# Which pairs of an input projection take seven products, and which stage forms their weight sums

## The chip, the cores and the metric

The kernel runs on one core of a Trainium2 chip. The metric is the device time of one execution in microseconds (us); a figure for a kernel is the median of its runs. The engines are TensorE (PE; its weight loads are listed apart as PEld), VectorE (DVE), ScalarE (ACT), GpSimd (POOL) and SyncE (SP). Each engine works through its own instructions in order and waits on semaphores for the others. Here SP issues the loads from memory and POOL most of the stores.

## The reference, cut to what matters

One inference step of a hybrid decoder over 1024 prompt tokens and 8 decoded tokens, model width 2048: one pooling layer (A), a shared key and value projection, one attention layer (B), all in float32. The change touches the input projection of layer A, `x @ w_in` with a weight of 2048 x 4096. Its first 2048 columns, here called the means, go through trailing means over 2, 4, 8 and 16 tokens in four channel groups of 512; its last 2048 columns are the gates.

```python
def multiscale_pool(u, prefix, pos):
    ...
    for g, w in enumerate(POOL_WINDOWS):
        ...
        outs.append((hi[..., sl] - lo) / cnt)
    pooled = jnp.concatenate(outs, axis=-1) - extf[:, P:]
    return pooled.astype(u.dtype), ext[:, -P:]

def pool_layer(x, prefix, pos, w_in, w_grp, scale, w_out, g_ln, b_ln):
    B, T, _ = x.shape
    z = x @ w_in
    u, gate = z[..., :D_POOL], z[..., D_POOL:]
    d, new_state = multiscale_pool(u, prefix, pos)
    d = jnp.einsum('btgc,gce->btge', d.reshape(B, T, N_POOL_GROUPS, POOL_GROUP), w_grp)
    d = d.reshape(B, T, D_POOL) * scale
    y = (d * jax.nn.silu(gate)) @ w_out
    return layer_norm(ALPHA * x + y, g_ln, b_ln), new_state
```

## The kernel before

**Stages.** The tokens go in two chunks (`c`): the first 512, then the other 512 with the 8 decoded ones (520). `PHASES` lists the stages: `ai` (input projection of A) for chunk 0 and 1, `ao` (output projection) for both, then `bi` and `bo` for layer B. `ai` of chunk 0 is cut in two entries: group 0 alone, and groups 1 to 3. Within a group come two pairs of means, two pairs of gates, and two group halves (`group_half`, the small product with `w_grp`, L1092, evicted by DVE at L1109).

**Exact products.** Each float32 operand is split in an upper half (a cast on ACT, L483 for weights, L773 for x) and a lower half (a subtraction on DVE, L498 for weights, L782 for x). A product takes three matmuls: upper by upper, upper by lower, lower by upper (L662, L663, L664 in seven-product form; L690, L691, L692 in plain form). A weight piece is 128x1024, 512 KB, loaded by SP.

**Plain and seven products.** A pair is two blocks of 128 output channels over all 2048 inputs and one chunk of tokens, so four weight pieces a11, a12, a21, a22. In plain form (`unit`, L1153 evicts a unit of the means on ACT, L1140 one of the gates) it is 4 entries of 24 matmuls with 512 columns. In the form of Strassen and Winograd (`seven`) it is 7 entries of 24 matmuls with half the columns, 256 or 260. Those need four sums of weight pieces and four sums of x tiles (T1 to T4). `PLAIN` names the stages in plain form: group 0 of `ai` in chunk 0, and half of `bi` in chunk 0. All others take seven products.

**Where the sums come from.** In a plain stage `plain_pair` loads the four pieces and afterwards forms the four weight sums on DVE (L288), which POOL stores (L289) for the second chunk. In a seven-product stage of chunk 0 `first_pair` forms them ahead of use (L341) from five loads (a22 twice) and stores them (L342). In chunk 1 `next_pair` loads seven pieces, four of them stored sums. The T tiles of the first chunk are formed from the plain stage's x tiles by `t_first` (L740 to L743, four operations for each quarter) at steps 3, 6, 9 and 12; two of the seven x operands are views of the plain tiles. The rest, ten pieces, are cast and split by `x_make` and `x_cast`, which `x_tick` calls at each step. `x_begin` starts this for the next stage; for the first seven-product stage it is called ahead of group 0's gates.

**Order.** One Python program writes the instructions, and a rule at the end (`in_order`) holds PE, DVE and ACT to the order in which they were written. `begin` looks ahead of each entry: loads 7 entries ahead, casts 4, lower halves 3 (5, 4 and 3 in a plain stage). A step (`end`) is one entry, or half of one in a plain stage. It runs what was due at that step (`at`), then `x_tick`, then now and then one step of background work (`side`). Background work is here `t_gen`, which loads x and writes T tiles of the next chunk (L830 to L833), `sum_gen`, which forms weight sums for the output projection, and the layer norms; how often it runs is counted in steps from the start of the program (`self.i / self.every`). In `ai` of chunk 0 five such steps are also put into each group's second pair of gates.

**A pool tile.** When a unit of the means is done, ACT copies it (L1153, or within `seven` the lines L601 to L635), DVE forms the trailing mean (L1038, L1046, L1049), ACT casts the result (L270) and DVE takes its lower half (L271).

The functions that the change touches, with the line numbers of the profile:

## Time and profile before

| | |
|---|---|
| median of 3 runs | 2331.8 us (2331.34 to 2332.02) |
| profiled execution, its own time | 2329.57 us |
| its span, first to last instruction | 2327.8 us |
| mean granted TensorE clock | 0.998 |
| busy share of the span | PE 99%, PEld 95%, DVE 83%, ACT 59%, POOL 9% |
| memory traffic | 669.26 MB, mean 288 GB/s |

A row of a timeline gives start, duration, engine, line, operation, output and input with their shapes, and in brackets how long the engine had been idle ahead of it and what ended that. Starts of successive rows on one engine lie a little closer than the durations, so the distance between starts is what an operation costs a busy engine. A window row gives busy time and instruction count of each engine, the granted TensorE clock (1.00 is full), the mean busy share of the DMA engines and GB/s. A list of waits gives who waited for whom, total, times, and the longest.

### The profile page before, as it was taken

What the parts mean: (1) busy time and instruction counts of PE and PEld (TensorE: products, weight loads), DVE (VectorE), ACT (ScalarE), POOL (GpSimd) and SP (SyncE); (2) the same over time, 40 slices, a digit from 0 to 9 for tenths busy, and PEclk for the clock granted to TensorE, in tenths of its full rate; (3) what the DMA queues carried; (4) which work ended last, traced back from release to release, by engine and by line L of the source; (5) the groups of instructions that cost most, each with busy time, mean ns of one, the idle gap of its engine ahead of it and who ended that gap; (6) DMA issues with size and microseconds to landing.
All of it is one profiled execution on the core that took longest, in us unless ns stands there. A gap on an engine that the chain in (4) does not pass through costs nothing. (4 is left out here: it accounts for less than half of the span.)

```text
span 2327.8 us, 49646 instructions
## 1 busy us (share of the span) xinstructions
PE 2297.9 (99%) x19960; PEld 2201.7 (95%) x19960; DVE 1922.3 (83%) x2382; ACT 1362.7 (59%) x2502; POOL 204.0 (9%) x384
## 2 busy tenths in 40 slices
PE   8999999999999999999999999999999999999997
PEld 6899999999999999999888899999999999999997
DVE  8788898777878878878898898897777767889897
ACT  4444455544546546655465566785766778656565
POOL 0111110010000000000111111100000000010001
PEclk9999999999999999999999999999999999999999
DMA  8668789988889988898789766788777758799785
GB/s 293 220 232 303 258 301 355 332 304 290 310 304 318 343 282 318 317 359 311 275 312 372 265 240 229 245 317 286 251 258 234 237 175 299 250 362 376 264 323 185
DMA packets 252216, 669.26 MB, mean 288 GB/s; under 512 B 25904, under 2 KB 106704, under 8 KB 251984
## 3 DMA queue, kind: packets, MB, share of 16 engines
q1 hardware_dynamic: 206512, 501.00, 63.4%
q0 software_dynamic: 45472, 165.07, 18.2%
q8 instruction: 156, 2.56, 0.4%
q14 instruction: 76, 0.62, 0.1%
HBM read 470.88 MB, written 185.59 MB: 282 GB/s over the span
## 5 line engine op out<-in xcount | busy, mean ns | idle before, releaser
L662 PE MATMUL pD<-m,m 128*128 128x260 f32 (+1 forms) x4752 | 1345.7, 283 | 1.8 <-ACT pD L601 0.9
L664 PE MATMUL pD<-m,m 128*128 128x260 f32 (+1 forms) x4752 | 1339.6, 282 | 5.5 <-DVE m L498 5.4
L663 PE MATMUL pD<-m,m 128*128 128x260 f32 (+1 forms) x4752 | 1340.0, 282 | 0.6 <-DVE m L782 0.6
L662 PEld LDWEIGHTS pD<-m,m 128*128 128x128 f32 x4752 | 895.5, 188 | 9.6 <-issue 5.5
L664 PEld LDWEIGHTS pD<-m,m 128*128 128x128 f32 x4752 | 895.9, 189 | 7.2 <-DVE m L498 7.1
L663 PEld LDWEIGHTS pD<-m,m 128*128 128x128 f32 x4752 | 895.6, 188 | 1.3 <-DVE m L782 0.8
L498 DVE TENSOR_TENSOR m<-m,m 128x1024 fp32r<-128x1024 f32 x674 | 814.6, 1220 | 96.2 <-ACT m L483 62.6
L483 ACT CAST m<-m 128x1024 fp32r<-128x1024 f32 x674 | 703.3, 1048 | 208.2 <-DVE m L341 84.9
L690 PE MATMUL pD<-m,m 128*128 128x512 f32 x448 | 179.8, 401 | 8.1 <-ACT m L773 8.1
L691 PE MATMUL pD<-m,m 128*128 128x512 f32 x448 | 177.4, 396 | 0.5 <-DVE m L782 0.5
L692 PE MATMUL pD<-m,m 128*128 128x512 f32 x448 | 177.4, 396 | 0.0
L782 DVE TENSOR_TENSOR m<-m,m 128x1024 fp32r<-128x1024 f32 (+1 forms) x120 | 147.0, 1227 | 10.3 <-ACT m L773 8.7
L773 ACT CAST m<-m 128x1024 fp32r<-128x1024 f32 (+1 forms) x120 | 125.8, 1052 | 14.0 <-DVE m L498 4.8
L341 DVE TENSOR_TENSOR m<-m,m 128x1024 f32<-128x1024 f32 x88 | 107.6, 1223 | 9.1 <-DMA m<-in_wia 6.8
L635 ACT COPY m<-pD 128x260 f32<-128x260 f32 (+1 forms) x83 | 31.0, 373 | 140.5 <-PE pD L664 140.2
L690 PEld LDWEIGHTS pD<-m,m 128*128 128x128 f32 x448 | 84.8, 189 | 29.4 <-ACT m L773 8.1
L623 DVE TENSOR_TENSOR m<-pD,m 128x260 f32<-128x260 f32 (+1 forms) x86 | 36.2, 421 | 83.8 <-ACT pD L622 76.3
L691 PEld LDWEIGHTS pD<-m,m 128*128 128x128 f32 x448 | 84.9, 189 | 20.0 <-DVE m L782 1.0
L692 PEld LDWEIGHTS pD<-m,m 128*128 128x128 f32 x448 | 84.8, 189 | 19.7
L1818 ACT ACTIVATE m<-m,sm 128x128 f32<-128x128 f32 x256 | 99.3, 391 | 0.0
L1092 PE MATMUL pD<-m,m 128*128 128x260 f32 (+1 forms) x528 | 91.2, 323 | 0.0
L1092 PEld LDWEIGHTS pD<-m,m 128*128 128x128 f32 x528 | 79.4, 188 | 8.1
(248 smaller groups left out, 2113.1 us busy)
## 6 DMA issues: line engine op xcount, KB each, us to landing
m<-in_wia SPq DMA_DIRECT2D x124, 512.0 KB
m<-in_wib SPq DMA_DIRECT2D x120, 512.0 KB
swia<-m POOLq DMA_DIRECT2D x64, 512.0 KB, 4.9
m<-swia SPq DMA_DIRECT2D x64, 512.0 KB
m<-swoa SPq DMA_DIRECT2D x64, 512.0 KB
swib<-m POOLq DMA_DIRECT2D x64, 512.0 KB, 5.1
m<-swib SPq DMA_DIRECT2D x64, 512.0 KB
m<-swob SPq DMA_DIRECT2D x56, 512.0 KB
```

What stands on the lines that cost most here:

```text
L341: self.nc.vector.tensor_add(s[out].a[:, :1024], s[x].a[:, :1024], s[y].a[:, :1024])
L483: self.nc.scalar.copy(hi.r[:, :1024], self.stream[self.cast].src().a[:, :1024])
L498: self.nc.vector.tensor_sub(lo.r[:, :1024], s.src().a[:, :1024], hi.a[:, :1024])
L662: nc.tensor.matmul(ps[:, :TH], wh[:, s], h, start=new and k == 0, stop=False, skip_group_check=on)
L663: nc.tensor.matmul(ps[:, :TH], wh[:, s], l, start=False, stop=False, skip_group_check=on)
L664: nc.tensor.matmul(ps[:, :TH], wl[:, s], h, start=False, stop=k == 7, skip_group_check=on)
L690: nc.tensor.matmul(ps[:], wh[:, s], h, start=par == 0 and k == 0, stop=False)
L691: nc.tensor.matmul(ps[:], wh[:, s], l, start=False, stop=False)
L692: nc.tensor.matmul(ps[:], wl[:, s], h, start=False, stop=par == 1 and k == 7)
L773: self.nc.scalar.copy(h.r[:, :n], s.a[:, :n])
L782: self.nc.vector.tensor_sub(l.r[:, :n], s.a[:, :n], h.a[:, :n])
L1092: nc.tensor.matmul(ps[:, : cs.stop - cs.start], ws[:, s], d[:, cs], start=f0 and k == 0, stop=l0 and k == 3,)
```

## The change

The first entry of `PHASES` now stands for the means of group 0 alone: parts are numbered 2g for the means of group g and 2g + 1 for its gates, so the first stage is part 0 and the second parts 1 to 7. The means of group 0 stay plain, by `bare_pair`, which forms no sums. Group 0's gates become the first two pairs of the second stage, with seven products and `first_pair`, which stores their sums for chunk 1 as for the other groups. In chunk 1 the means of group 0, its first two pairs, no longer find stored sums; `first_pair` with `keep=False` forms them there from five loads and stores nothing. `phase_ai` is cut into `means` and `gates`. The quarters of T tiles are formed at steps 3, 5, 7 and 9, and `x_begin` for the second stage is called at step 10 of the first stage's 16, with `turn` set, so that `x_tick` handles two pieces a step.

```diff
--- before.py
+++ after.py
@@ -48,7 +48,7 @@
 N_CST = K_MP + P + 1
 
 PHASES = (
-    ("ai", 0, (0, 1)), ("ai", 0, (1, 4)), ("ai", 1, (0, 4)), ("ao", 0, None), ("ao", 1, None), ("bi", 0, (0, 4)),
+    ("ai", 0, (0, 1)), ("ai", 0, (1, 8)), ("ai", 1, (0, 8)), ("ao", 0, None), ("ao", 1, None), ("bi", 0, (0, 4)),
     ("bi", 0, (4, 8)), ("bi", 1, (0, 8)), ("bo", 0, None), ("bo", 1, None),
 )
 PHASE_OF = {"x": "ai", "g": "ao", "h": "bi", "o": "bo"}
@@ -324,7 +324,12 @@
             ent[i].loads.insert(0, lambda: self.sums(name, q))
         return ent
 
-    def first_pair(self, name, q):
+    def bare_pair(self, name, q):
+
+        a11, a12, a21, a22 = self.quads(name, q)
+        return [self.lone(a) for a in (a11, a12, a21, a22)]
+
+    def first_pair(self, name, q, keep=True):
 
         a11, a12, a21, a22 = self.quads(name, q)
         ws = self.ws[name][q]
@@ -339,12 +344,13 @@
                 if out not in s:
                     s[out] = self.mem.full(1024)
                 self.nc.vector.tensor_add(s[out].a[:, :1024], s[x].a[:, :1024], s[y].a[:, :1024])
-                self.nc.gpsimd.dma_start(ws[:, i, :], s[out].a[:, :1024])
+                if keep:
+                    self.nc.gpsimd.dma_start(ws[:, i, :], s[out].a[:, :1024])
 
             return go
 
         def free(*ks):
-            return [lambda k=k: s.pop(k).free(k != "c") for k in ks]
+            return [lambda k=k: s.pop(k).free(keep and k != "c") for k in ks]
 
         ent = lambda k, loads, make, after: Entry(loads, make, lambda: s[k], after)
         return {
@@ -374,10 +380,17 @@
             if seven and c == 0:
                 pr = lambda name, q: (lambda f: [f[i] for i in ORDER7])(self.first_pair(name, q))
             if kind == "ai":
-                for g in range(*part):
-                    for q in (2 * g, 2 * g + 1, 8 + 2 * g, 9 + 2 * g):
-                        w += pr("wia", q)
-                    for h in range(2):
+                for n in range(*part):
+                    g, gates = divmod(n, 2)
+                    for q in (8 * gates + 2 * g, 8 * gates + 2 * g + 1):
+                        if n:
+                            w += pr("wia", q)
+                        elif c == 0:
+                            w += self.bare_pair("wia", q)
+                        else:
+                            f = self.first_pair("wia", q, False)
+                            w += [f[i] for i in ORDER7]
+                    for h in range(2 if gates else 0):
                         w.append(self.lone(io["wg"][g][:, h * 1024 : (h + 1) * 1024]))
             elif kind == "bi":
                 if part[0] == 0:
@@ -1133,18 +1146,19 @@
 
         return box, z(0), z(1)
 
-    def phase_ai(self, c, gs, nxt):
+    def phase_ai(self, c, parts, nxt):
         nc, io = self.nc, self.io
         T = CHUNKS[c][1]
         TH = T // 2
         silu = lambda dst, ps: nc.scalar.activation(dst, ps, AF.Silu)
-        for g in gs:
+
+        def means(g, end):
             ext = es = None
             if T > TP:
                 es = self.mem.half(T)
                 ext = es.a[:, :512].rearrange("p (i b w) -> p i b w", i=4, b=NDEC)
                 nc.sync.dma_start(ext, io["st"][:, 4 * g : 4 * g + 4])
-            dd, sg = {}, {}
+            dd = self.dd = {}
             for i in range(4):
                 if not self.strassen:
 
@@ -1153,6 +1167,7 @@
                         nc.scalar.copy(U.a[:, NST : NST + T], ps[:])
                         self.at(1, lambda: self.pool_tile(c, 4 * g + i, U, None, dd))
 
+                    self.last = end and i == 3
                     self.unit(done)
                 elif i % 2 == 0:
                     us = {}
@@ -1170,6 +1185,7 @@
                         self.at(n + 4, lambda: self.pool_tile(c, 4 * g + i + 1, us[1], ext, dd))
 
                     self.pair(c, z(0), z(1), done)
+            self.last = False
             if ext is not None:
 
                 def put(es=es, ext=ext, g=g):
@@ -1177,35 +1193,31 @@
                     es.free()
 
                 self.at(8, put)
-            for i in range(4):
-                if g == gs[-1] and i == 0:
-                    self.x_begin(nxt)
-                if not self.strassen:
-
-                    def done(ps, i=i):
-                        if i % 2 == 0:
-                            sg[i // 2] = self.mem.full(2 * T)
-                        silu(sg[i // 2].a[:, (i % 2) * T : (i % 2 + 1) * T], ps[:])
-
-                    self.last = g == gs[-1] and i == 3
-                    self.unit(done)
-                elif i % 2 == 0:
-                    box, z0, z1 = self.two(T)
-
-                    def done(i=i, box=box):
-                        s = box["s"]
-                        silu(s.a[:, TH : 2 * T], s.a[:, TH : 2 * T])
-                        sg[i // 2] = s
-
-                    if c == 0 and i == 2:
-
-                        for n in range(0, 10, 2):
-                            self.at(n, lambda: self.side and self.side_step())
-                    self.last = g == gs[-1] and i == 2
-                    self.pair(c, z0, z1, done, silu)
+
+        def gates(g, end):
+            sg = {}
+            if end:
+                self.x_begin(nxt)
+            for i in (0, 2):
+                box, z0, z1 = self.two(T)
+
+                def done(i=i, box=box):
+                    s = box["s"]
+                    silu(s.a[:, TH : 2 * T], s.a[:, TH : 2 * T])
+                    sg[i // 2] = s
+
+                if c == 0 and i == 2:
+
+                    for n in range(0, 10, 2):
+                        self.at(n, lambda: self.side and self.side_step())
+                self.last = end and i == 2
+                self.pair(c, z0, z1, done, silu)
             self.last = False
             for h in range(2):
-                self.group_half(c, g, h, dd, sg)
+                self.group_half(c, g, h, self.dd, sg)
+
+        for n in parts:
+            (gates if n % 2 else means)(n // 2, n == parts[-1])
         if T > TP:
             nc.sync.dma_start(io["npp"], self.carry)
 
@@ -2116,8 +2128,8 @@
             if n == 3:
                 self.prep_to(2)
         for j in range(4):
-            self.at(3 + 3 * j, lambda j=j: self.t_first(j))
-        self.at(13, lambda: setattr(self, "x0", None))
+            self.at(3 + 2 * j, lambda j=j: self.t_first(j))
+        self.at(10, lambda: setattr(self, "x0", None))
         nc.vector.tensor_scalar(
             self.nsink, self.nsink, -1.0, None, op0=ALU.mult
         )
@@ -2160,7 +2172,8 @@
             self.at(7, lambda: setattr(self, "turn", False))
             self.at(13, lambda: setattr(self, "lock", False))
             if n == 0:
-                pass
+                self.at(10, lambda: self.x_begin(1))
+                self.at(10, lambda: setattr(self, "turn", True))
             elif (kind, c) == ("ai", 0):
                 add(("x", 1, False), self.t_gen(("x", 1)))
                 self.room = 99
```

What moves is shown at three places. The lines of the code before are 13 lower than those after from L495 on (L498 is L511, L782 is L795, L773 is L786, L483 is L496, L270 and L271 stay, L341 is L346, L1109 is L1122, L1153 is L1167).

On DVE, around the end of group 0's means, before: the sums of the plain stage (L288) between lower halves of plain gates, and the first x pieces of the seven-product stage (L782).

```order
L498 TENSOR_TENSOR m_83_586<-m_71_508,m_78_548 128x1024
L288 TENSOR_TENSOR m_71_508<-m_67_464,m_71_508 128x1024
L271 TENSOR_TENSOR m_85_604<-m_81_580,m_85_604 128x512
L288 TENSOR_TENSOR m_67_464<-m_54_380,m_67_464 128x1024
L498 TENSOR_TENSOR m_89_628<-m_76_544,m_84_588 128x1024
L288 TENSOR_TENSOR m_54_380<-m_54_380,m_71_508 128x1024
L782 TENSOR_TENSOR m_91_646<-m_79_562,m_86_621 128x1024
L288 TENSOR_TENSOR m_62_424<-m_54_380,m_62_424 128x1024
L782 TENSOR_TENSOR m_93_664<-m_80_564,m_92_648 128x1024
L498 TENSOR_TENSOR m_96_670<-m_82_584,m_90_630 128x1024
```

And after, from the last operation of the third unit's pool tile (L1062) on:

```order
L1062 TENSOR_SCALAR m_72_494<-m_72_494,m_69_460 128x512
L511 TENSOR_TENSOR m_76_504<-m_63_422,m_71_466 128x1024
L346 TENSOR_TENSOR m_62_420<-m_58_380,m_62_420 128x1024
L346 TENSOR_TENSOR m_58_380<-m_58_380,m_63_422 128x1024
L271 TENSOR_TENSOR m_78_524<-m_72_494,m_78_524 128x512
L795 TENSOR_TENSOR m_79_527<-m_67_443,m_73_498 128x1024
L795 TENSOR_TENSOR m_80_529<-m_68_445,m_74_500 128x1024
L795 TENSOR_TENSOR m_83_547<-m_41_286,m_81_531 128x1024
L795 TENSOR_TENSOR m_84_549<-m_54_370,m_82_533 128x1024
L511 TENSOR_TENSOR m_89_559<-m_58_380,m_77_510 128x1024
L795 TENSOR_TENSOR m_91_588<-m_40_285,m_85_551 128x1024
L795 TENSOR_TENSOR m_92_590<-m_53_369,m_86_553 128x1024
```

The sums of the first gate pair (L346) and the x pieces (L795, two by two) now stand here, next to the means' pool tiles, and the split L271 has a sum directly ahead of it.

On ACT at the same place, before: the fourth unit's eviction (L1153) behind the split of the third unit's tile (L270).

```order
L483 COPY m_73_512<-m_67_464 128x1024
L270 COPY m_74_526<-m_70_504 128x512
L1153 COPY m_75_542<-pD_461 128x512
L483 COPY m_78_548<-m_71_508 128x1024
L1030 COPY area<-m_75_542 128x15
L483 COPY m_84_588<-m_76_544 128x1024
L270 COPY m_85_604<-m_81_580 128x512
L773 COPY m_86_621<-m_79_562 128x1024
L1140 ACT_TABLE_LOAD
```

And after, from the third unit's eviction (L1167) on:

```order
L1167 COPY m_69_460<-pD_377 128x512
L496 COPY m_71_466<-m_63_422 128x1024
L1043 COPY area<-m_69_460 128x15
L786 COPY m_73_498<-m_67_443 128x1024
L786 COPY m_74_500<-m_68_445 128x1024
L496 COPY m_77_510<-m_58_380 128x1024
L270 COPY m_78_524<-m_72_494 128x512
L786 COPY m_81_531<-m_41_286 128x1024
L786 COPY m_82_533<-m_54_370 128x1024
```

Ahead of the split L270 there are now two x casts (L786) and the cast of a weight sum (L496, `m_58_380`, which the second sum of the fence above writes, in the row behind `m_62_420`).

On DVE at the end of chunk 0's `ai`, where the group halves of group 3 are evicted (L1109, from `pD`), before:

```order
L498 TENSOR_TENSOR m_490_4082<-m_466_3933,m_485_4046 128x1024
L782 TENSOR_TENSOR m_492_4112<-m_460_3896,m_487_4074 128x1040
L1109 TENSOR_SCALAR m_495_4118<-pD_4086,prm,m_433_3698 128x512
L1109 TENSOR_SCALAR m_495_4118<-pD_4099,prm,m_433_3698 128x512
L498 TENSOR_TENSOR m_497_4124<-m_471_3967,m_491_4084 128x1024
L782 TENSOR_TENSOR m_499_4154<-m_465_3930,m_493_4114 128x1040
L1109 TENSOR_SCALAR m_503_4162<-pD_4128,prm,m_470_3965 128x512
L1109 TENSOR_SCALAR m_503_4162<-pD_4141,prm,m_470_3965 128x512
```

And after:

```order
L511 TENSOR_TENSOR m_500_4218<-m_478_4074,m_495_4183 128x1024
L346 TENSOR_TENSOR m_488_4143<-m_487_4141,m_488_4143 128x1024
L795 TENSOR_TENSOR m_502_4247<-m_475_4068,m_497_4211 128x1040
L511 TENSOR_TENSOR m_505_4255<-m_482_4107,m_501_4220 128x1024
L346 TENSOR_TENSOR m_487_4141<-m_482_4107,m_487_4141 128x1024
L346 TENSOR_TENSOR m_482_4107<-m_482_4107,m_488_4143 128x1024
L795 TENSOR_TENSOR m_507_4287<-m_476_4070,m_503_4249 128x1040
L1122 TENSOR_SCALAR m_510_4293<-pD_4261,prm,m_449_3872 128x512
L1122 TENSOR_SCALAR m_510_4293<-pD_4274,prm,m_449_3872 128x512
L511 TENSOR_TENSOR m_511_4297<-m_488_4143,m_506_4257 128x1024
L795 TENSOR_TENSOR m_513_4327<-m_481_4104,m_508_4289 128x1040
```

Three of the sums for group 0's means in chunk 1 (L346) come ahead of the first group half's evictions (L1122).

## The prediction

> **What bounds the kernel now.** I read the page's first and fifth parts, then TensorE's own list of waits, then windows over the stages that the change touches, and last single rows there.
>
> The page:
> ```profile
> PE 2297.9 (99%) x19960; PEld 2201.7 (95%) x19960; DVE 1922.3 (83%) x2382; ACT 1362.7 (59%) x2502; POOL 204.0 (9%) x384
> ...
> L498 DVE TENSOR_TENSOR m<-m,m 128x1024 fp32r<-128x1024 f32 x674 | 814.6, 1220 | 96.2 <-ACT m L483 62.6
> ...
> L341 DVE TENSOR_TENSOR m<-m,m 128x1024 f32<-128x1024 f32 x88 | 107.6, 1223 | 9.1 <-DMA m<-in_wia 6.8
> ```
> TensorE's waits (us in total, times, longest):
> ```profile
> PE pD L690 <- ACT m L773: 8.1, 1, 8.1
> PE pD L664 <- DVE m L498: 5.4, 7, 2.9
> PE pD L662 <- ACT pD L601: 0.9, 1, 0.9
> ```
> PE is busy for 2297.9 of 2327.8 us. Past the start-up wait of 8.1 us little is left to gain but matmuls themselves, and a wait on any other engine lengthens the end by its own length. Of those waits, the one that recurs is for DVE's lower weight halves (L498).
>
> Stretches of 40 us (PE, PEld, DVE, ACT, POOL, granted clock, DMA share, GB/s): the plain group, the rest of it, a settled stretch of seven products, and the start of the second token chunk.
> ```profile
> 20.00:60.00 40.00, 40.00 (x175) 32.47 (x174) 39.32 (x51) 15.90 (x25) 4.68 (x10) 1.00 0.77 274
> 60.00:100.00 40.00, 40.00 (x174) 32.48 (x173) 30.04 (x27) 18.55 (x20) 4.26 (x8) 1.00 0.53 185
> 220.00:260.00 40.00, 40.00 (x342) 40.00 (x341) 37.58 (x45) 20.02 (x33) 4.84 (x11) 1.00 0.57 209
> 380.00:420.00 40.00, 40.00 (x303) 38.49 (x302) 34.14 (x50) 20.77 (x31) 3.43 (x7) 1.00 0.99 355
> 420.00:460.00 40.00, 40.00 (x336) 40.00 (x335) 31.75 (x52) 21.64 (x39) 3.36 (x6) 1.00 0.93 346
> ```
> PE never pauses in any of them. DVE is the engine next to the bound: full at 20 to 60 us, with 10 us to spare at 60 to 100, 6 at 380 to 420 and 8 at 420 to 460.
>
> **What the change removes from TensorE.** The two gate pairs of group 0 go from 96 matmuls of 512 columns each to 168 of 256. Each form's price is a distance on ACT between evictions that waited for PE: two successive plain units (L1153), and the first and second pair of a group (L601).
> ```profile
> 45.18 0.59 ACT L1153 COPY m<-pD 128x512 f32<-128x512 f32 x1 [1.25 <-PE pD L692]
> ...
> 56.27 0.59 ACT L1153 COPY m<-pD 128x512 f32<-128x512 f32 x1 [0.73 <-PE pD L692]
> ...
> 134.51 0.37 ACT L601 ACTIVATE pD<-pD 128x256 f32<-128x256 f32 x1 [1.36 <-PE pD L664]
> 154.32 0.37 ACT L601 ACTIVATE pD<-pD 128x256 f32<-128x256 f32 x1 [1.52 <-PE pD L664]
> ```
> A plain unit takes 11.09 us, so a pair 22.18; a pair of seven products 19.81 (0.118 us a matmul). The gain is 2.37 a pair, **4.74 us** for both. It can't be more: everything else that moves is off PE.
>
> The weight loads are busy for all 40 us at 220 to 260 and for 32.5 in the plain stretches, so in seven products they are level with the matmuls. The page "TensorE: Matmul & The Clock Gate" of the Trainium skill, section Back-to-back issue gap, goes further: it gives sustained spacings of about 81 ns at 128 columns and 131 ns at 512; an estimate between them puts 256 columns near 98 ns, a plain pair at 12.6 us and seven products at 16.4, so by it the change loses some 7.7 us. The trace here has 231 and 118 ns, and the measurement decides. What such a bound by weight loads would do by rows is a rival below.
>
> **What else leaves and comes.** *Sums.* Group 0 formed 16 sums with 16 stores of 512 KB (L288, L289); now the gates form 8 with 8 stores, and the means' 8 are formed at the start of the second chunk and not stored. Eight DVE adds (1.13 us each, the distance between such rows) leave a full DVE at 20 to 60 us, where PE waited for none of them: 0. Eight stores leave POOL, 9% busy: 0. *Loads.* Two more on SP's queue for the gates (DMA share 0.53 at 60 to 100: hidden), four fewer in the second chunk, where the share is 0.99 and 0.93: no wait of PE in the list above is for a load, so 0; below that a gain of at most what sums waited for loads in the whole run, 6.8 us in the L341 row, of which PE saw nothing. *Casts.* Six more pieces on ACT and six more lower halves on DVE, in the gates. ACT is at 18.55 of 40 there: 0 by volume, though its order matters below. *Side steps.* Five steps of the background generator move from group 2 to group 1, and from 1 to 0; three of their four-operation groups come into group 0's gates. They stand behind the start-up chain below, where I find DVE ahead of PE again: 0.
>
> **The first seven-product pair.** This is where the gain is partly paid back. Before, the ten x pieces (L773, L782) were made among plain gates over some 50 us; now they are due within seven entries right after the means. Rows that carry the sum:
> ```profile
> 32.21 0.69 DVE L1038 TENSOR_TENSOR m<-m 128x512 f32<-128x512 f32 x1
> 32.93 0.16 DVE L1046 TENSOR_TENSOR m<-m,cst 128x1 f32<-128x1 f32 x1
> 33.13 0.69 DVE L1049 SCALAR_TENSOR_TENSOR m<-m,m 128x512 f32<-128x512 f32 x1
> 33.74 1.22 DVE L498 TENSOR_TENSOR m<-m,m 128x1024 fp32r<-128x1024 f32 x1
> ...
> 45.59 0.68 DVE L271 TENSOR_TENSOR m<-m,m 128x512 fp32r<-128x512 f32 x1
> 46.20 1.22 DVE L288 TENSOR_TENSOR m<-m,m 128x1024 f32<-128x1024 f32 x1
> 47.33 1.22 DVE L498 TENSOR_TENSOR m<-m,m 128x1024 fp32r<-128x1024 f32 x1
> ...
> 49.60 0.69 DVE L740 TENSOR_TENSOR m<-m 128x512 f32<-128x512 f32 x1
> ...
> 52.14 1.22 DVE L288 TENSOR_TENSOR m<-m,m 128x1024 f32<-128x1024 f32 x1
> ```
> ```profile
> 46.72 1.05 ACT L483 CAST m<-m 128x1024 fp32r<-128x1024 f32 x1
> 54.91 0.62 ACT L270 CAST m<-m 128x512 fp32r<-128x512 f32 x1 [7.15 <-DVE m L1049]
> ```
> ```profile
> 56.07 0.39 PE L690 MATMUL pD<-m,m 128*128 128x512 f32 x1
> ```
> So a 1024-wide operation costs 1.13, a pool tile 1.53 (32.21 to 33.74), its split 0.61, and one quarter of the first T tiles 2.54 (49.60 to 52.14). I carry the order of DVE after the change (quoted ahead) forward with these. The split L271 at 45.59 has five L288 ahead of it (less 5.7), and now the fourth quarter of T tiles too (plus 2.5); with the split and the lower half behind it (1.7) DVE stands at 44.1, or 43.75 with the small waits between followed one by one. Then come four adds, five lower weight halves, ten x halves, two pool tiles and two splits up to the lower half of the sixth gate entry: 19 x 1.13 + 2 x 1.53 + 2 x 0.61 = 25.8, so 69.5 if nothing waits. Two waits are certain from the order. The pool tile of the third unit needs ACT's copy of that unit, ready at 45.7 (45.18 + 0.5): 0.85 lost. And the split of that tile needs ACT's L270, which stands behind the cast of a sum that DVE has only just added: add done at 50.85, cast 1.05, L270 0.6, so the split starts at 52.55 and DVE idles 1.7. Together 2.55, so about 72.
>
> PE begins the gates at 56.07. The fifth entry's lower half is first read after 4 x 24 + 2 matmuls at 0.118, at 67.6; it is ready at about 68.5. The sixth is read at 70.4, or 71.4 with that delay, and ready at 72.5. Stall 0.95 + 1.15 = **2.1 us**. For the second pair's first entry I get 76.35 ready against 78.3 needed, then 1.0 us to spare, then more. Bounds: 0 if the two DVE idles shrink (25.8 us without them is in time), and up to 5 us if another ACT cast joins the chain of add, cast, L270, split, about 2.9 us a turn.
>
> What a pause does to the clock is in these windows:
> ```profile
> 356.00:360.00 4.00, 1.46 (x10) 1.46 (x11) 3.93 (x7) 2.58 (x4) 0.00 (x0) 0.93 1.03 403
> 360.00:364.00 4.00, 4.00 (x25) 4.00 (x25) 3.97 (x5) 3.52 (x6) 0.00 (x0) 0.64 0.90 318
> 730.00:735.00 5.00, 4.07 (x34) 3.87 (x33) 5.00 (x6) 5.00 (x8) 0.00 (x0) 1.00 0.98 326
> ```
> One wait of 2.9 us was followed by a clock of 0.64: 25 matmuls instead of 34 in 4 us, so 9 x 0.118 = 1.1 us, which I take as 1.5 since 0.93 stands in the window ahead. A pause of 0.9 us left it at 1.00. My two stalls are of the second size: no clock term. The Trainium skill's same page, in its part on the HAM clock gate, says that half rate follows at least one idle window of about 3.4 us; the row above dropped after 2.9, so the safe length is shorter here than that rule says. By rule or row, two stalls of 1 us add nothing.
>
> **The second chunk's sums.** At its start two pairs gain four adds each, 9.0 us of DVE. There DVE waits for the group halves:
> ```profile
> 379.88 0.75 DVE L1109 SCALAR_TENSOR_TENSOR m<-pD,prm,m 128x512 f32<-128x512 f32 x1 [0.38 <-PE pD L1092]
> 382.64 0.75 DVE L1109 SCALAR_TENSOR_TENSOR m<-pD,prm,m 128x512 f32<-128x512 f32 x1 [2.02 <-PE pD L1092]
> ...
> 388.20 0.75 DVE L1109 SCALAR_TENSOR_TENSOR m<-pD,prm,m 128x512 f32<-128x512 f32 x1 [1.86 <-PE pD L1092]
> ```
> The idles are 0.38 + 2.02 + 1.86 = 4.26 us, which takes in nearly four adds; the other four fall on a stretch where DVE has 8 of 40 free. Carrying the order forward, the lower halves come 0.7 to 1.2 us ahead of need and the fourth entry of the second pair 0.3 late: **+0.3**, between 0 and 9.0 (all eight exposed).
>
> **Later phases.** Two steps fewer shift the points at which background work runs. Near 2156 two small DVE operations move ahead of two halves (at most 1.2 us if they are read at once), near 2264 another moves the other way, where one stall of under 1 us might go. Net 0, bounds -0.9 and +1.2.
>
> **Sum.** -4.74 + 2.1 + 0.3 = -2.3 us. The profiled execution took 2329.57, 2.2 under the median of the runs shown, 2331.8 (2331.34 to 2332.02); on the median this gives **2329.5**, in a profile 2327.2. The bound of the chances, 0.2% of the median, is 4.66 us: 2327.1 and 2336.5.
>
> **Rivals.**
> *All of it shows, 2327.0.* The DVE idles shrink, no lower half is late, and later reordering removes a stall: 2331.8 - 4.74, down to 2326.1 with the -0.9. For it: 25.8 us fit without idles, and a margin of 1 us either way decides. Against it: ACT's order.
>
> *The second chunk's adds are exposed, 2338.* One mechanism: the eight adds sit ahead of lower halves on DVE, which works in order, so each late half holds PE, and with it the evictions that DVE waits for. Price 8 x 1.13 = 9.0 in place of my 0.3: 2331.8 - 4.74 + 2.1 + 9.0 = 2338.2. It needs over 7.3 us of the 9.0 to show before the end is slower by the bound. Against it: 4.26 us of idle rows, and 34.14 + 31.75 + 9.0 = 74.9 of 80 us. For it: DMA at 0.99 there, and a sum needs two loads to have landed.
>
> *The first pair stalls in one piece, 2334.* If the two late halves and the ACT chain add up to one pause like that of 356 us, 5 us + 1.5 of slow clock replace 2.1: 2333.9. Still within the bound. Point of decision: a pause of near 2.9 us.
>
> *The gates don't get cheaper, 2334.2.* If weight loads bound seven products, group 0's gates would cost what plain ones do, and only 2.1 + 0.3 would remain. Against it: groups beside it run this very form at 0.118. The Trainium skill's spacing rule above is a harsher form of it.
>
> **Chances.** My forecast's case (part of the gain paid back) 0.52; all of it 0.22; exposed adds 0.10; one long stall 0.10; no cheaper gates 0.03; a clash of the shifted background work beyond its bound 0.03. Faster by over 0.2%: 0.20, nearly all of the second case. Slower by over 0.2%: the adds, 0.10, the clash, 0.03, and 0.04 of the long stall, where another follows it: 0.17. Within: 0.63. Within 0.2% is about what a measurement of this kernel can't tell from no change. Range 2325.8 (all, with the -0.9) to 2337.5 (most adds exposed).
>
> **What the profile after would show.** L690 x384 instead of x448 (448 less two pairs of 32), and gates of group 0 at 19.8 us between L614's first evictions (the line that L601 becomes). DVE idle near 51 to 52.5 before L271, then PE waits on L511 (now L498) of about 1 us twice at 67 to 73, clock 1.00. In the second chunk, idles before L1122 gone at 380 to 390, PE waits of under 1 us near 420. The group 3 stall of 2.9 us stays, 2.6 us earlier. I am wrong if a pause over 2.5 us with a clock below 1 stands near 70 or 420, or if a wait appears on a load from DMA.

## The result and the profile after

The changed kernel takes 2343.2 us (median of 6 runs, 2342.12 to 2346.4) against 2331.91 (6 runs, 2331.34 to 2333.67) on the same chip. The ratio on record is 1.0044, with a 95% interval of 1.0035 to 1.0054 (the quotient of the medians is 1.0048). It is 11.3 us slower; 2.3 us faster was forecast, and the range ended at 2337.5.

The page of the changed kernel, the rows that answer to those shown of before:
```profile
span 2343.7 us, 49895 instructions
...
PE 2297.3 (98%) x20104; PEld 2206.8 (94%) x20104; DVE 1930.2 (82%) x2392; ACT 1372.2 (59%) x2518; POOL 199.6 (9%) x376
...
L346 DVE TENSOR_TENSOR m<-m,m 128x1024 f32<-128x1024 f32 x104 | 127.1, 1222 | 4.8 <-DMA m<-in_wia 2.2
```
PE's busy time has hardly changed while the span has grown by 15.9 us (the profiled execution was one of 2345.45 us): PE's idle time grew by 16.5 us. But the busy time was to fall by the 4.74 us of cheaper matmuls, and it fell by 0.6. The rest is mostly clock: twice, behind 1160 and behind 1720 us, the granted clock is 0.83 over 10 us, by an estimate 1.7 us each, where it is 1.00 in the kernel before. (L346 has 16 more operations than L341 had, and L288, not shown, 16 fewer.) The head of TensorE's list of waits in the changed kernel, us in total, times, longest:
```profile
PE pD L677 <- DVE m L511: 9.4, 9, 4.3
PE pD L703 <- ACT m L786: 8.0, 1, 8.0
PE pS L1794 <- DVE m L1764: 3.8, 2, 2.0
PE pO L1871 <- DVE m L1857: 3.3, 3, 2.1
PE pD L663 <- ACT m L648: 2.3, 1, 2.3
PE pS L1718 <- ACT m L2043: 2.0, 1, 2.0
PE pO L1871 <- ACT m L1856: 1.8, 1, 1.8
```
All but the first two lie in layer B, whose code the change doesn't touch, and most of them in its attention. (Behind `phase_ai` the lines after are 12 higher than before, so L1706 is L1718 and L1636 is L1648. In runs with one more line above they are one higher again.)

Where the time went is seen best from a difference of two timelines. From group 1 on both kernels issue the same matmuls in the same order, so a matmul can be found in both by counting from the last one. This is its start in a kernel less its start in the kernel before, in us, at the times (in the kernel before) at the head:

```
at                     130    340    400    450    770   1110   1140   1180   1360   1540   1740   1830   2130   2310
the changed kernel    -2.6   -2.2   -0.2    0.5   -0.1    0.1    1.9    5.5    7.0    7.7   11.4   15.0   17.6   15.6
```

By 130 us the change stands at -2.6. By the end of layer A, at 1110 us, it has lost that again and stands even. The whole of the slowdown, 15.5 us in this execution, arises in layer B. A row of this table compares two single executions. Executions of one kernel spread by some 7 us (27 of the kernel before: 2330.25 to 2337.44), and the trace of before is one of its shorter ones, so a difference of 1 or 2 us says little by itself.

The first pair of seven products, row by row in the changed kernel, on DVE and on PE:
```profile
45.74 0.69 DVE L1051 TENSOR_TENSOR m<-m 128x512 f32<-128x512 f32 x1 [0.88 <-ACT m L1167]
52.52 0.69 DVE L271 TENSOR_TENSOR m<-m,m 128x512 fp32r<-128x512 f32 x1 [1.64 <-ACT m L270]
```
```profile
68.54 0.38 PE L677 MATMUL pD<-m,m 128*128 128x256 f32 x1 [0.90 <-DVE m L511]
72.55 0.39 PE L677 MATMUL pD<-m,m 128*128 128x256 f32 x1 [0.91 <-DVE m L511]
```
The two DVE idles (0.88 and 1.64) and the two PE waits (0.90 and 0.91) are those of the forecast (0.85, 1.7; 0.95, 1.15), in their places.

In group 3 a DVE sum waits for a weight load, and PE then for DVE; before and after:
```profile
346.95 1.23 DVE L341 TENSOR_TENSOR m<-m,m 128x1024 f32<-128x1024 f32 x1 [0.34 <-DMA m<-in_wia]
358.54 0.39 PE L664 MATMUL pD<-m,m 128*128 128x256 f32 x1 [2.94 <-DVE m L498]
```
```profile
346.06 1.23 DVE L346 TENSOR_TENSOR m<-m,m 128x1024 f32<-128x1024 f32 x1 [1.80 <-DMA m<-in_wia]
357.65 0.39 PE L677 MATMUL pD<-m,m 128*128 128x256 f32 x1 [4.26 <-DVE m L511]
```
The load cost DVE 1.80 us in place of 0.34, and PE waited 4.26 in place of 2.94. The order on DVE is the same here in both kernels. DVE reached the sum 2.35 us earlier than before, and the load landed only 0.9 us earlier. In all 2.0 us of the lead went.

Layer B, first place, near 1130 us. PE before and after:
```profile
1129.54 0.98 PE L1706 MATMUL pS<-cst,m 128*128 128x128 f32 x7 [0.22 <-ACT m L2031]
```
```profile
1131.45 0.98 PE L1718 MATMUL pS<-cst,m 128*128 128x128 f32 x7 [2.03 <-ACT m L2043]
```
PE waits for an eviction on ACT. It stands behind a layer norm operation of ACT (L982), which waits 2.36 us for DVE, where the new order puts two more operations ahead. The table goes from 0.1 to 1.9.

Second place. DVE before (its row for the layer norm's statistics, which a matmul into `pO` forms):
```profile
1141.93 0.43 DVE L983 TENSOR_SCALAR m<-pO 128x260 f32<-128x260 f32 x1 [0.46 <-PE pO L887]
```
and after, with PE a little later, and the clock around it, after and in the last row before (windows: PE, PEld, DVE, ACT, POOL, clock, DMA share, GB/s):
```profile
1146.62 0.43 DVE L996 TENSOR_SCALAR m<-pO 128x260 f32<-128x260 f32 x1 [4.44 <-PE pO L900]
```
```profile
1159.89 0.37 PE L1794 MATMUL pS<-m,m 64*32 64x160 f32 x8 [2.00 <-DVE m L1764]
```
```profile
1150.00:1160.00 10.00, 8.00 (x43) 6.24 (x49) 9.93 (x12) 5.81 (x7) 1.68 (x4) 1.00 0.60 218
1160.00:1170.00 10.00, 10.00 (x96) 7.96 (x93) 9.79 (x13) 3.75 (x5) 2.59 (x5) 0.83 0.95 337
```
```profile
1160.00:1170.00 10.00, 10.00 (x44) 8.09 (x44) 9.80 (x10) 6.53 (x22) 1.59 (x3) 1.00 0.94 373
```
The statistics matmul (L900, before L887) starts 4.7 us later, at 1146.17 against 1141.49; 1.9 us were lost ahead of it, and 2.8 are its later place in PE's own order. DVE stands idle for 4.44 us until it is done, and what stands behind on DVE is the operation that the first attention scores need (L1764). PE waits 2.00 us for it, and the clock falls to 0.83 over the next 10 us.

Third place: the partner copies, four transfers from tile to tile for the rotary embedding, on SP's queue. SP and DVE before, then SP after:
```profile
1691.12 2.49 SPq L1636 DMA_DIRECT2D m<-m  x4
1700.50 2.40 DVE L1644 TENSOR_TENSOR m<-m,m 128x1040 f32<-128x1040 f32 x2 [0.27 <-DMA m<-m]
```
```profile
1704.84 0.34 SPq L282 DMA_DIRECT2D m<-in_wib  x1
1705.27 2.53 SPq L1648 DMA_DIRECT2D m<-m  x4
```
and what SP and DVE waited for there in the changed kernel:
```profile
SPq L282 <- DMA swob<-m: 8.1, 1, 8.1
```
```profile
1711.81 2.39 DVE L1656 TENSOR_TENSOR m<-m,m 128x1040 f32<-128x1040 f32 x2 [4.75 <-DMA m<-m]
```
A weight load (L282) was given a tile whose own store (`swob`) hadn't landed. SP waited 8.1 us, and the partner copies stood behind it. DVE's rotary embedding (L1656) then waited 4.75 us, against 0.27 before. In the table the next 3.7 us are lost there, between 1540 and 1740: PE waits 2.05 us at 1718 (L1871), and the clock is 0.83 from 1720 to 1730. Over the whole kernel DVE waits 19.4 us for these copies, before 10.7.

### The profile page after: what moved, and what is told of

The parts are those of the page before. It is cut to its first block, busy times and chain, and to the rows that moved or that the text cites. A ratio compares the mean times of both kernels' runs of the same rounds, so it can differ in the third digit from the quotient of the medians.

```text
span 2343.7 us, 49895 instructions
## 1 busy us (share of the span) xinstructions
PE 2297.3 (98%) x20104; PEld 2206.8 (94%) x20104; DVE 1930.2 (82%) x2392; ACT 1372.2 (59%) x2518; POOL 199.6 (9%) x376
## 4 chain that ended last, share of the span: by engine, by line
PE 76%; DVE 6%; DMA 3%; issue 2%; ACT 2%; SPq 0%; POOL 0%; DVEq 0%; ACTq 0%; POOLq 0%
PE pD L675 19%; PE pD L677 19%; PE pD L676 19%; PE pD L703 3%; PE pD L1105 3%; PE pD L705 3%; PE pD L704 3%; PE pO L1871 2%; PE pS L1794 2%; DVE m L511 2%; PE pS L1847 1%; DMA m<-m 1%; DVE m L1051 1%; DMA m<-in_wia 1%; DMA m<-swoa 1%
## 5 line engine op out<-in xcount | busy, mean ns | idle before, releaser
L677 PE MATMUL pD<-m,m 128*128 128x260 f32 (+1 forms) x4864 | 1371.4, 282 | 9.4 <-DVE m L511 9.4
L675 PE MATMUL pD<-m,m 128*128 128x260 f32 (+1 forms) x4864 | 1377.2, 283 | 1.5 <-ACT pD L614 1.4
L676 PE MATMUL pD<-m,m 128*128 128x260 f32 (+1 forms) x4864 | 1370.9, 282 | 0.9 <-DVE m L795 0.9
L677 PEld LDWEIGHTS pD<-m,m 128*128 128x128 f32 x4864 | 917.0, 189 | 11.4 <-DVE m L511 11.4
L675 PEld LDWEIGHTS pD<-m,m 128*128 128x128 f32 x4864 | 916.5, 188 | 9.6 <-issue 5.9
L676 PEld LDWEIGHTS pD<-m,m 128*128 128x128 f32 x4864 | 917.0, 189 | 1.7 <-DVE m L795 1.1
L511 DVE TENSOR_TENSOR m<-m,m 128x1024 fp32r<-128x1024 f32 x680 | 821.0, 1219 | 103.0 <-ACT m L496 67.7
L496 ACT CAST m<-m 128x1024 fp32r<-128x1024 f32 x680 | 709.5, 1048 | 223.4 <-DVE m L346 87.0
L703 PE MATMUL pD<-m,m 128*128 128x512 f32 x384 | 154.8, 403 | 8.0 <-ACT m L786 8.0
L704 PE MATMUL pD<-m,m 128*128 128x512 f32 x384 | 152.3, 397 | 0.7 <-DVE m L795 0.7
L705 PE MATMUL pD<-m,m 128*128 128x512 f32 x384 | 152.1, 396 | 0.0
L795 DVE TENSOR_TENSOR m<-m,m 128x1024 fp32r<-128x1024 f32 (+1 forms) x120 | 146.3, 1224 | 4.1 <-ACT m L786 2.5
L786 ACT CAST m<-m 128x1024 fp32r<-128x1024 f32 (+1 forms) x120 | 125.3, 1052 | 12.1 <-DVE m L511 4.4
L346 DVE TENSOR_TENSOR m<-m,m 128x1024 f32<-128x1024 f32 x104 | 127.1, 1222 | 4.8 <-DMA m<-in_wia 2.2
L703 PEld LDWEIGHTS pD<-m,m 128*128 128x128 f32 x384 | 72.9, 190 | 26.8 <-ACT m L786 8.0
L614 ACT ACTIVATE pD<-pD 128x260 f32<-128x260 f32 (+1 forms) x86 | 31.8, 370 | 106.9 <-PE pD L677 106.4
L1105 PE MATMUL pD<-m,m 128*128 128x260 f32 (+1 forms) x528 | 91.2, 323 | 0.0
L704 PEld LDWEIGHTS pD<-m,m 128*128 128x128 f32 x384 | 73.0, 190 | 17.7 <-DVE m L795 1.8
L705 PEld LDWEIGHTS pD<-m,m 128*128 128x128 f32 x384 | 72.8, 189 | 16.9
```

The lines of the kernel that those rows point to most:

```text
L346: self.nc.vector.tensor_add(s[out].a[:, :1024], s[x].a[:, :1024], s[y].a[:, :1024])
L496: self.nc.scalar.copy(hi.r[:, :1024], self.stream[self.cast].src().a[:, :1024])
L511: self.nc.vector.tensor_sub(lo.r[:, :1024], s.src().a[:, :1024], hi.a[:, :1024])
L675: nc.tensor.matmul(ps[:, :TH], wh[:, s], h, start=new and k == 0, stop=False, skip_group_check=on)
L676: nc.tensor.matmul(ps[:, :TH], wh[:, s], l, start=False, stop=False, skip_group_check=on)
L677: nc.tensor.matmul(ps[:, :TH], wl[:, s], h, start=False, stop=k == 7, skip_group_check=on)
```

## The experiments

Two theories. T: background work in layer B falls on other steps, because the change's first stages have two steps fewer and the pace is counted from the program's start. S: the change leaves tiles free in another order, so loads in layer B get tiles whose stores are late, and what stands behind them on SP's queue comes late. Each ratio is to the runs of the kernel before on the same chip, with its 95% interval.

**The counter alone, both ways.** The changed kernel with its counter two higher, and the kernel before with its counter two lower:

```diff
         self.i = self.e = self.lastO = self.turns = self.ring = 0
+        self.i = 2      # the other kernel: self.i = -2
```

> The changed kernel with the step counter started at 2 instead of 0, so that from the second stage on background work falls on the same steps as in the kernel before. Theory (the loss is made in layer B by the counter standing two steps lower there): the 15.6 us lost between 1100 us and the end go, and the time is 2328 to 2332. Rival (the loss comes from what the change leaves behind, tiles in other slots, loads in another order, no stored sums for two pairs): the counter doesn't matter and the time stays near 2343.

> The kernel before with the step counter started at -2, nothing else. Theory: layer B loses as in the changed kernel, 2343 to 2348. Rival: 2332, as the kernel before.

Measured: the changed kernel 2334.94 (1.0002, 0.9994 to 1.0011), the kernel before 2347.64 against 2333.58 (1.0056, 1.0040 to 1.0072). A kernel that differs from before by the counter alone loses as much as the change. With the counter put right the slowdown is gone, though the median is some 3 us above the theory's window. Its row in the table further down says where: at 1110 us it stands at 3.1, the changed kernel at 0.1. So by these two traces the lower counter was worth 3 us in layer A (0.9 in the kernel before, by the row of e2), and only in layer B did it cost.

**Each half of the change alone.** Seven products for group 0's gates, with the first stage still forming and storing its sums; and the second chunk's sums with group 0 plain throughout. The edit of the first (the counter also starts at 2):

```diff
                         elif c == 0:
-                            w += self.bare_pair("wia", q)
+                            w += self.plain_pair("wia", q)
                         else:
-                            f = self.first_pair("wia", q, False)
-                            w += [f[i] for i in ORDER7]
+                            w += pr("wia", q)
```

> Group 0's gates take seven products as in the change, but the plain means form and store their sums in the first stage and the second chunk loads them as before; the counter starts at 2. Theory: the gain of 4.7 less the start-up stalls of some 2 us, less 2.1 us lost again near 360 us in group 3: 2329 to 2332. Rival (the loss follows the gates): above 2340.

The edit of the second, shortened (`bare_pair` and `keep` are as in the change):

```diff
                     for q in (2 * g, 2 * g + 1, 8 + 2 * g, 9 + 2 * g):
-                        w += pr("wia", q)
+                        if q > 1:
+                            w += pr("wia", q)
+                        elif c == 0:
+                            w += self.bare_pair("wia", q)
+                        else:
+                            f = self.first_pair("wia", q, False)
+                            w += [f[i] for i in ORDER7]
```

> The kernel before (plain gates of group 0, counter unchanged), but the means of group 0 form no sums in the first stage and the second chunk forms them as in the change. Theory: only the second chunk's own cost shows, 0.3 forecast and 0.7 read from the trace of the changed kernel: 2332 to 2333. Rival (the loss follows the sums that are no longer stored): above 2340.

Measured: 2343.54 (1.0042, 1.0027 to 1.0057) and 2337.25 (1.0010, 1.0001 to 1.0020). The first comes out where its rival put it, but not for the rival's reason: there is a cause in its own stage. PE at 50 to 100 us in that kernel:
```profile
PE pD L676 <- DVE m L795: 6.9, 1, 6.9
PE pD L677 <- DVE m L511: 1.7, 2, 0.9
```
and its clock:
```profile
60.00:70.00 10.00, 6.83 (x44) 6.83 (x45) 8.71 (x9) 10.00 (x14) 0.53 (x1) 0.66 0.64 224
```
With the sums left in a full first stage PE waits 6.9 us for an x piece, the clock is 0.66 over 10 us, and the kernel stands at +6.1 by 130 us instead of -2.6, and at 9.1 by the end of layer A. The two halves of the change belong together: taking the sums out is what makes the seven products affordable. The second misses both windows. It costs 2.1 us around 420 us by its trace (its row below goes from -0.7 to 1.4), not 0.3. Then, though DVE, ACT and PE have exactly the order of before in layer B, its profiled execution loses some 8 us more there. 5.8 of them go between 1660 and 1680 us: SP had waited 6.5 us for a store (`swob`) ahead of the partner copies, DVE waited 7.0 for the copies, PE 3.1 for DVE, and the clock fell.
```profile
DVE m L1656 <- DMA m<-m: 16.0, 5, 7.0
```
That is what S says. But this execution, 2340.20 us, was the slowest of eleven, and the ratio puts this kernel only 2.3 us above the one before, so such a clash needn't happen in each of them.

**The tiles alone, the partner copies alone, and the pace of layer B alone.**

```diff
             self.c, self.ph = c, kind + str(c)
+            if (kind, c, part) == PHASES[5]:
+                for _ in range(4):
+                    f = self.mem.f
+                    i = min(self.mem.whole(), key=lambda i: max(f[i]))
+                    self.mem.clock += 1
+                    f[i] = [self.mem.clock, self.mem.clock]
```

> The kernel before, with the four longest free tiles of the pool put to the end of the line at the start of layer B; no instruction of PE, DVE or ACT changes its place, only which tile a load gets, and so what it waits for. Theory S (layer B loses time where a load on SP's queue gets a tile whose store hasn't landed, and the partner copies for the rotary embedding wait behind it): the time moves by 3 us or more from that of before, to either side. Theory T (only the step at which background work falls matters): no change, within 1.5 us.

> The same turn of four free tiles in the changed kernel. S: moves by 3 us or more from 2343. T: 2343, within 1.5 us.

The first edit is to the kernel before, the second is the same in the changed kernel. Measured: before with turned tiles 2338.54 against 2333.69 (1.0017, 1.0008 to 1.0025), the changed kernel 2343.34 (1.0038, 1.0025 to 1.0052), about as without the turn (1.0044). The first is as S has it: 4.0 us by the ratio, 4.9 between the medians, where no instruction of PE, DVE or ACT moved, and DVE's waits for partner copies went from 10.7 to 23.1 us. The second didn't move, as T has it; where the counter is off, another order of tiles is no worse. DVE's waits for partner copies fell there from 19.4 to 12.8 us without a gain, so their total alone doesn't set the time.

```diff
-        if self.side and int(self.i / self.every) != int((self.i - 1) / self.every) and room >= self.room:
+        j = self.i + (2 if self.ph[0] == "b" else 0)
+        if self.side and int(j / self.every) != int((j - 1) / self.every) and room >= self.room:
```

> The changed kernel, with the two missing steps added to the count that paces background work, from layer B on only. T: the 15 us of layer B go, 2328 to 2331. S: the order of DVE goes back to that of before, but the tiles do not, so a part of the loss stays: 2332 to 2340.

```diff
-            self.nc.sync.dma_start(t.a[32 * a : 32 * a + 32, : n * T], s.a[32 * b : 32 * b + 32, : n * T])
+            self.nc.scalar.dma_start(t.a[32 * a : 32 * a + 32, : n * T], s.a[32 * b : 32 * b + 32, : n * T])
```

> The changed kernel, with the partner copies (four of 130 KB each time, tile to tile, ahead of the rotary embedding) issued from ACT's queue instead of SP's, so that no load waiting for a tile stands ahead of them. S: DVE's 19.4 us of waits for them (L1656) fall below 8, and with them most of the PE waits at L1794 and L1871: 2330 to 2338. T: no gain, 2342 to 2346.

Measured: with the pace of layer B put right **2330.66 against 2333.69 (0.9989, 0.9980 to 0.9997)**, faster than before by about 2.6 us. That is T's window; S's, 2332 to 2340, missed: hardly any loss of layer B is left over for the tiles to explain (the row of e7 below). The partner copies on ACT's queue: 2340.30 (1.0029, 1.0020 to 1.0038), DVE's waits for them 7.8 instead of 19.4 us, as expected. PE's waits at L1794 and L1871 fell from 8.9 to 3.6 us. But the time falls by some 3 us only and stays above the theory's window: other waits came (L675 for ACT, 3.0 us in place of 1.4), and the edit itself puts issues on ACT, whose cost wasn't separated. By this run the late copies are a part of the loss, and not the larger.

**Which stage of layer B.** The same two steps given only to the plain half of `bi` in chunk 0, only to the stages behind it, and one step too many given to the kernel before (`self.k` is the stage's number in `PHASES`, and `j` takes the place of `self.i` in the next line, as above):

```diff
+        j = self.i + (2 if self.k == 5 else 0)     # the second: self.k > 5; the kernel before: 1 if self.k > 4
```

> The changed kernel with the two steps added to the count only in the plain half of layer B's input projection (about 1090 to 1350 us), where the key and value projection, its layer norm steps and the first attention products lie. If background work out of place there makes the loss, directly (6.6 us by 1350 us in the changed kernel's trace) and by the tiles and loads that it leaves for the stages behind (8.4 us more): 2329 to 2333. If each stage pays for its own count: only the 6.6 us go, 2336 to 2338.

> The complement: the two steps added only in the stages behind that half. If the plain half makes the loss: the 6.6 us up to 1350 us stay and most of the rest, 2340 to 2344. If each stage pays for its own count: 2334 to 2337.

> The kernel before with one step added to the count from layer B on. If layer B was fitted to the count that it has (any shift costs): slower by 4 us or more, 2338 to 2348. If only the lower count hurts (work that comes later than its user needs it): within 2 us of before, 2332 to 2335.

Measured: **2328.69 against 2331.69 (0.9987, 0.9979 to 0.9996)**; 2343.20 (1.0043, 1.0029 to 1.0057); 2343.97 (1.0053, 1.0040 to 1.0066). The first window holds: the pace in one stage of some 260 us decides the whole loss, also that behind it. The last fits its first case, that layer B was fitted to the count it had: one step more costs as much as two fewer. No other shift was tried.

The same difference of timelines for these, and for three runs from above:

```
at                     130    340    400    450    770   1110   1140   1180   1360   1540   1740   1830   2130   2310
e7  pace of layer B   -2.5   -2.1   -0.8    0.2   -0.4   -0.2   -0.7   -0.7    0.3   -0.2    0.9    0.9    2.2    0.7
e9  of its 1st stage  -2.5   -2.1   -0.8   -0.1   -0.8   -0.6   -1.0   -1.0    0.0   -0.8    0.6    0.6   -0.2   -2.5
e10 of the others     -2.6   -2.2    0.2    1.0    0.3    0.5    2.3    5.9    6.0   10.3   11.2   15.7   17.0   16.9
e1  counter at 2      -2.5   -2.1    0.6    2.8    3.0    3.1    3.7    3.7    4.1    3.2    5.2    5.5    6.8    6.6
e2  before, 2 fewer   -0.1   -0.1   -0.5   -0.5   -1.1   -0.9    1.2    3.2    4.5    8.7    8.9   12.8   15.6   15.3
e4  sums alone        -0.2    0.1   -0.7    1.4    1.8    2.0    1.8    1.8    2.0    2.2    8.2    8.1   10.6    9.8
e5  before, turned    -0.1    0.0   -0.8   -0.8   -0.8   -0.8    0.7    0.7    1.6    1.5    4.5    4.5    7.4    5.9
e11 before, 1 more    -0.1   -0.1    0.4    0.4    0.4    0.4    2.7    2.7    4.6   10.6   14.0   16.0   20.4   20.1
```

With the pace right layer B is flat to within some 3 us, and PE's waits behind 1000 us in the kernel of e9 are, the longest three,
```profile
PE pD L1517 <- DVE m L1474: 1.7, 1, 1.7
PE pO L1872 <- DVE m L1858: 1.6, 1, 1.6
PE pD L677 <- DVE m L796: 0.9, 1, 0.9
```
and DVE's wait for the statistics is short again:
```profile
1140.90 0.43 DVE L997 TENSOR_SCALAR m<-pO 128x260 f32<-128x260 f32 x1 [0.47 <-PE pO L901]
```

## Why the prediction was wrong

The failed step is the term "Later phases": "Two steps fewer shift the points at which background work runs ... Net 0, bounds -0.9 and +1.2." It was worth about 13 us (the ratio 1.0044 of the changed kernel against 0.9989 with the pace of layer B put right: 0.0055 of 2332). It looked at two places in the last stage, where operations of DVE change order, and priced them by the length of what moves ahead, at most 1.2 us. For these two places that held: e9 keeps their changed order and loses nothing there (-0.2 at 2130, -2.5 at 2310). It did not look at 1090 to 1270 us, where DVE's order changes as well. What a shift cost there was set by what the displaced work waits for: a step of layer norm that comes late on PE holds DVE for 4.44 us, and behind it the attention. And it took instruction order as all that a shift changes. Which tile a load gets changes too; e5 shows that alone to be worth 4 to 5 us.

Point by point:
- *The gain on PE and the first seven-product pair.* -4.74 + 2.1 = -2.6 us forecast by then, -2.6 measured at 130 us. Right in its cause, its places and its size; the clock stayed at 1.00 there as argued.
- *Group 3's stall "stays".* Wrong: 2.94 became 4.26 us, because DVE, which had no slack, waited 1.46 us longer for a weight load, and 2.0 us of the lead went (1.3 to 2.7 between 340 and 400 us in e1 and e6 to e10, where the stall is 3.0 to 3.9). The step "no wait of PE in the list above is for a load, so 0", taken for the second chunk's loads, was not safe as a rule: here a load that DVE waits for became one that PE waits for, by way of DVE.
- *The second chunk's sums.* +0.3 forecast; 0.7 in the changed kernel (the table from 400 to 450), 1.0 in e7, 2.1 in e4 and 2.2 in e1, the two with the background work of layer A in its old place. Within its bounds, and under-sized. DVE's idles ahead of the group halves shrank from 4.26 to 0.44 us, as forecast. The rival of 2338, all eight adds exposed, didn't happen, although the measured time came out beyond it.
- *One stall of PE near 730 us* (0.9 us, for ACT's L601) vanished, which none of the terms had: some 0.7 gained. It goes with the counter: e2 gains it too, and e1 doesn't.
- *The sum without the later phases.* With the pace of layer B put right the times are 2.6 (e7; 0.9989 of 2333.69) and 3.0 us (e9; 0.9987 of 2331.69) under the kernel before, each with about 2 on either side, and -2.3 was forecast. That agreement is in part luck. By the table both kernels have paid the gain back by 1110 us (-0.2 and -0.6; the changed kernel 0.1), to group 3, whose stall was to stay as it was, and to the second chunk, which took more than its term. Where the 2 to 3 us between the medians come from the traces don't show; that of before is of an execution 2.2 us below its median.
- *The side that says slower* had the clash of shifted background work at a chance of 0.03. It was the case that came, with a price some ten times its bound. (The other end of the range, 2325.8, is 0.3 to 0.4 below what its words add up to, 2331.8 - 4.74 - 0.9; nothing hangs on it.)

What is shown: that the pace in the first stage of layer B makes the loss (e2, e7, e9, e10), and that another order of tiles alone costs some us in the kernel before (e5). What was only read from traces: that the losses behind that stage, 8.6 of the 15.6 us, come through tiles and late loads. DVE's order is the same there from about 1270 to 1800 us, the SP row at 1704.84 is such a case, and so is e4 at 1660; e8 takes away a part. Against a larger part speaks e6, where the turned tiles shortened the waits for the copies and not the time. How much goes which way, and how much of it is the clock behind a wait, wasn't separated.

## What to carry to other kernels

Where background work is paced by a counter from the program's start, adding or dropping a step re-times all that is behind. Give a stage that was fitted to its count that count back, and look at the others one by one: here layer A was 1 to 3 us better off with the lower count. Before costing a shift at the length of what moved, ask what the moved work waits for and who stands behind it on the same in-order engine or queue. A difference of two timelines by matched matmuls tells in one table which stage lost the time; here it isn't one that was changed.

## What the runs showed that I had not expected

The tile that an allocator picks is part of the schedule: four free tiles put to the end of the line, with every instruction of PE, DVE and ACT in its place, cost 4 to 5 us (a ratio of 1.0017). And a pause of PE of 2.00 us at 1160 us was followed by a clock of 0.83 over 10 us, where pauses of 0.90 and 0.91 us at 68 and 72 us left it at 1.00; in the trace of before, the one pause behind which the clock falls in mid-kernel is 2.94. But the length doesn't settle it in this region: 2.03 us at 1131 us in the same execution, and 2.49 us at 1132 in e11, left the clock at 1.00.
